# Two heads' attention scores on the two row halves of the matrix array, in a two-layer float32 trunk

## The chip, the core and the metric

One core of a Trainium2 chip runs the whole program. The metric is the device time of one execution in microseconds (us). The engines are PE (matrix products; its weight loads are listed as PEld), DVE and ACT (elementwise work; both read PE's accumulator banks), POOL (small elementwise work here) and SP, which issues the transfers. Every engine takes its instructions in the order in which the program lists them. Products land in accumulator banks, of which the kernel keeps eight of 128 x 512 float32.

## The reference

A trunk of two layers over 256 tokens of width 1024, all in float32. Layer 0 mixes tokens with eight stick-breaking heads and four differential heads (two softmax maps each), layer 1 with sixteen heads whose block choice, at 256 tokens, leaves plain causal softmax. All heads have 64 features, so a "pair" below is two heads (or the two maps of a differential head). Behind each mixer stand a squared-ReLU MLP and a gated embedding.

```python
z = jnp.einsum('bhqd,bhkd->bhqk', qi, k) * scale          # stick-breaking scores
s = jnp.einsum('bhqd,bhkd->bhqk', qi, ki) * scale         # each map of a differential head
s_own = jnp.einsum('bhqd,bhkd->bhqk', qi, k_own) * scale  # layer 1
...
h = h + squared_relu_mlp(rms_norm(h, mlp_norm[i]), w_ff1[i], w_ff2[i])
gate = jax.nn.sigmoid(rms_norm(h, ple_norm[i]) @ ple_gate[i])
h = h + gate * (p[i].astype(h.dtype) @ ple_proj[i])
```

There are 16 pairs: four stick-breaking, four differential, eight in layer 1.

## The kernel before

**Products.** A float32 product is made of three products in the format fp32r: each operand is split exactly into a high and a low part, and `mm3` issues high x high, high x low and low x high into one bank. Weights stream from memory in units of half a megabyte (`raw`), ACT writes their high part (`whi`), DVE the low part (`wlo`). The tokens stand as transposed activations `T0h`, `T0l`, `T1h`, `T1l`. Almost all of PE's work is this stream; attention is set between its products.

**Order.** Nothing is scheduled by the chip: a planner (`Order`) runs the tasks as generators, keeps a clock for each engine from cost formulas, and issues next the task of the highest rank whose wait is over by those clocks. So a changed cost or a changed wait in one task moves instructions of others too. Banks are taken from a pool of eight; side work such as attention holds at most five of them in layer 0 (`banks.room`).

**Scores.** Queries and keys of a pair lie on 128 partitions, head 0 on partitions 0 to 63 and head 1 on 64 to 127. A product over 128 partitions would add the two heads up. So one operand is kept zero-padded: the tiles `z` (high) and `zl` (low) are [128, pair, head, 256 tokens], and head 0's copy is zero on partitions 64 to 127, head 1's on 0 to 63. POOL writes the zeros (`z_tile`, lines 1184 and 1185), and the sinks `qk_sink` and `T_sink` write the two halves in two instructions of 64 partitions on ACT and again on DVE. A single product then gives both heads side by side in one bank.

- `soft` (a query tile t of 128 rows): t = 0 gives 2 x 128 columns, t = 1 gives 2 x 256, three products each. `diff_head` and `moba_pair` call it for t = 0 and t = 1 in turn; each call takes a bank, and DVE reads it (line 781) before the bank is given back.
- `stick_pair` (rows are keys): three products of 512 columns, a mask product in bfloat16 (256 columns), three of 256, another mask. Later it adds running sums of the softplus terms `sph`, `spl` by six products with the constant `negr`: two of 512 columns and four of 256.
- `average` (line 165) multiplies weights by values for two heads on the two column halves of the array: the tile is 128 rows by 64 columns, the two heads' products stand in turn in PE's list. It is plain float32, and each product appears as two records in the trace.

**The start.** POOL's list begins with the identity, then the zeros of layer 0, then the rotary tables from the token positions (`table_task`, tile `posi`), the norms (`rs_a`), the mask constants and the rotations of the first queries and keys (`rp`, `tok`).

Of the kernel before, what the change touches and what calls it, by code (L numbers as in the profile page):

```python
# [17 lines left out]
P = 128  # L18
# [29 lines left out]
# ---- order of issue: tasks are generators that yield what they wait for; the one of the  # L48
# highest rank whose wait is over by the clocks of the engines issues next ----
# [5 lines left out]
class Buffers:  # L55
    """Buffers that tasks take and give back."""
# [26 lines left out]
class Order:  # L83
# [66 lines left out]
    # -- instructions, each returning when its result can be read --  # L150
# [62 lines left out]
    def copy(self, out, in_, ps=False, scale=None, dep=0.0):  # L213
        """On the engine that is through with it first."""
# [13 lines left out]
def kernel(  # L228
# [65 lines left out]
    def constants_task():  # L294
# [5 lines left out]
        # rows are queries, columns keys: a key after its query is out  # L300
# [169 lines left out]
    class Norm:  # L470
        """rs = 1/rms, rs8 = rs/8, rs2 = 1/rms^2 of each token tile"""
# [10 lines left out]
    def transposes(nm, t, c, dep, calm=False):  # L482
        """h[t][:, c] -> acts"""
# [28 lines left out]
    def statistics(nm, t, pieces, need):  # L512
        """pieces of the row: (first column, columns, event)"""
# [29 lines left out]
    def chunk(acts, sink, tmajor=False):  # L543
        """512 output features, token-major; sink(t, bank) is a task"""
# [29 lines left out]
    def chunk_T(acts, sink):  # L574
        """512 output features on partitions, 128 at a time; sink(f2, bank) is a task for two such blocks"""
# [22 lines left out]
    def qk_sink(nm, dst, ev, eighth, padded):  # L598
        def sink(t, bk, dep):
# [22 lines left out]
            ts_ = slice(t * P, (t + 1) * P)  # L622
# [16 lines left out]
    def rows_task(nm):  # L639
        """1/rms of each token along the columns, on every partition"""  # L640
# [9 lines left out]
    def T_sink(dst, evs_, eighth, padded):  # L650
        def sink(f2, bk, dep):
# [7 lines left out]
            js = slice(2 * f2, 2 * f2 + 2)  # L659
            if padded:  # L660
                parts = [(v[64 * g:64 * g + 64], [d[64 * g:64 * g + 64, js, g, :] for d in dst]) for g in range(2)]
            else:
                parts = [(v, [d[:, js, :] for d in dst])]
            for v_, (hi, lo) in parts:
                e = o.act(hi, v_, AF.Copy)
            yield e
            for v_, (hi, lo) in parts:
                e = o.tt(lo, v_, hi.bitcast(F32), ALU.subtract)
# [28 lines left out]
    def put_T(oo, dep, acts, j):  # L697
        """token-major oo [128, 2 x 128] -> 128 features of acts"""
# [14 lines left out]
    scores = [0, None]  # L713

    def scored():
        """a pair's scores are out"""
# [4 lines left out]
    def stick_pair(j, kT, qz, q_ev, k_ev, v, v_ev, acts):  # L721
        yield (q_ev[j // 2], k_ev[j // 2], mask_ev, big.wake)
        b1 = big.take()
        e = b1[1]
        yield lambda: banks.wake(2, side=True)
        ba, bb = banks.take(side=True), banks.take(side=True)
        pa, pb = ba[1], bb[1][:, :256]
        a3 = pa.rearrange("q (g n) -> q g n", g=2)
        b3 = pb.rearrange("q (g n) -> q g n", g=2)
# [5 lines left out]
        yield ea  # L735
        o.act(e[:, :512], pa, AF.Abs, ps=True)
        o.act(e[:, 512:], pb, AF.Abs, ps=True, dep=eb)
        o.act(e, e, AF.Exp, scale=-1.0)
        t = o.act(e, e, AF.Ln, bias=one)
        yield t  # L740
        o.stt(e[:, 512:], pb, 0.0, e[:, 512:], ALU.max, ALU.add)
        t = o.stt(e[:, :512], pa, 0.0, e[:, :512], ALU.max, ALU.add)
# [3 lines left out]
        t = o.act(sph, e, AF.Copy)  # L746
        yield t
        t = o.tt(spl, e, sph.bitcast(F32), ALU.subtract)
# [6 lines left out]
        sps.give(*b2, t2)  # L755
        yield t1
        t1 = o.act(e[:, :512], pa, AF.Exp, ps=True)
        t2 = o.act(e[:, 512:], pb, AF.Exp, ps=True)
        banks.give(*ba, t1, side=True)
        banks.give(*bb, t2, side=True)  # L760
        yield (t2, *v_ev)
        wa = e[:, :512].rearrange("q (g n) -> q g n", g=2)
        wb = e[:, 512:].rearrange("q (g n) -> q g n", g=2)
        yield from average(lambda g: wa[:, g, :], lambda g: wb[:, g, :], v, j * P, acts, j, b1)

# [1 line left out]
    def soft(j, t, qT, kz, q_ev, k_ev, e, st):  # L767
# [8 lines left out]
        if t == 1:  # L776
            scored()
# [509 lines left out]
```

## Time and profile before

| | |
|---|---|
| time, median of 3 runs (lowest to highest) | 676.93 us (676.45 to 677.07) |
| span of the profiled execution | 674.7 us |
| PE busy, share of the span | 656.8 us, 97% |
| PE weight loads | 569.6 us, 84% |
| DVE busy | 451.6 us, 67% |
| ACT busy | 417.1 us, 62% |
| POOL busy | 61.9 us, 9% |
| granted clock of PE, mean | 0.998 of full speed |

The span runs from the first to the last recorded instruction; no own time of the profiled execution stands beside it, and the median of the timed runs is 2.2 us longer than the span. A matmul record lasts longer than the step to the next one, since products are pipelined: what a product costs PE is read from the distance between the starts of records that follow each other, not from their durations.

### The profile page before, as it was taken

The page shows a single profiled execution, that of the slowest core. Times are in us where ns is not written, and L with a number is a line of the kernel's source. Part 1 is how long each engine was busy: PE and PEld are TensorE (multiplying, and loading weights), DVE is VectorE, ACT ScalarE, POOL GpSimd, SP SyncE. Part 2 cuts the span into 40 slices and gives each one's busy share as a digit, 9 for nine tenths or more (in the row PEclk, how much of TensorE's full clock was granted, in tenths as well). Part 3 has the DMA queues.
Part 4 walks back from the last instruction along what each step waited for, and adds up shares of the span by engine and source line. Part 5 has one row for each costly group of instructions (what it writes and reads, how often), then busy time and mean ns, then how long its engine had stood idle before and what let it go on. Part 6 is the DMA issues. An engine that isn't in the chain of part 4 may idle for free.

```text
span 674.7 us, 10997 instructions
## 1 busy us (share of the span) xinstructions
PE 656.8 (97%) x3906; PEld 569.6 (84%) x3906; DVE 451.6 (67%) x936; ACT 417.1 (62%) x886; POOL 61.9 (9%) x129
## 2 busy tenths in 40 slices
PE   6799999999999999999999999999999999999995
PEld 4589878899998999898887777778998999899885
DVE  6789767777456554666895776758657545655584
ACT  7667887675446553655796776758646544655482
POOL 8820001000000000000043022000000000000010
PEclk9999999999999999999999999999999999999999
DMA  7753643456466546754656434435476546654621
GB/s 256 219 202 93 199 130 114 133 170 227 150 223 218 169 153 210 229 173 140 198 184 197 139 113 145 156 94 176 146 242 207 167 149 226 219 169 150 211 95 62
DMA packets 50054, 115.61 MB, mean 171 GB/s; under 512 B 4000, under 2 KB 5456, under 8 KB 50000
## 3 DMA queue, kind: packets, MB, share of 16 engines
q1 hardware_dynamic: 49824, 114.39, 52.0%
q8 instruction: 30, 0.49, 0.3%
q0 software_dynamic: 176, 0.53, 0.3%
q14 instruction: 24, 0.20, 0.1%
HBM read 113.86 MB, written 1.05 MB: 170 GB/s over the span
## 4 chain that ended last, share of the span: by engine, by line
PE 83%; issue 8%; POOL 7%; ACT 0%; DVE 0%; POOLq 0%; DVEq 0%; ACTq 0%
PE bank L159 80%; POOL rp L196 3%; PE bank L170 2%; PE bank L165 1%; POOL tok L196 1%; POOL prod L1102 1%; POOL rem L1103 1%; ACT tok L178 0%; POOL zl L1184 0%; POOL z L1185 0%; POOL z L1184 0%; POOL zl L1185 0%; POOL ang L1092 0%; POOL rs_a L527 0%; POOL rs_f L527 0%
## 5 line engine op out<-in xcount | busy, mean ns | idle before, releaser
L192 DVE TENSOR_TENSOR wlo<-raw,whi 128x512 fp32r<-128x512 f32 x424 | 276.9, 696 | 89.1 <-ACT whi L178 63.5
L178 ACT ACTIVATE whi<-raw 128x512 fp32r<-128x512 f32 x424 | 243.7, 628 | 97.9 <-PE bank L159 71.9
L159 PE MATMUL bank<-T0h,whi 128*128 128x256 f32 x576 | 161.7, 281 | 0.0
L159 PE MATMUL bank<-whi,hid 128*128 128x512 f32 x512 | 161.4, 391 | 0.0
L159 PE MATMUL bank<-T0l,whi 128*128 128x256 f32 x576 | 160.8, 279 | 0.0
L159 PE MATMUL bank<-T0h,wlo 128*128 128x256 f32 x576 | 160.7, 279 | 0.0
L159 PEld LDWEIGHTS bank<-whi,hid 128*128 128x128 f32 x512 | 96.1, 188 | 19.7
L159 PEld LDWEIGHTS bank<-T0h,whi 128*128 128x128 f32 x576 | 108.2, 188 | 0.7
L159 PEld LDWEIGHTS bank<-T0l,whi 128*128 128x128 f32 x576 | 107.8, 187 | 0.7
L159 PEld LDWEIGHTS bank<-T0h,wlo 128*128 128x128 f32 x576 | 108.2, 188 | 0.0
L159 PE MATMUL bank<-wlo,hid 128*128 128x512 f32 x256 | 99.6, 389 | 0.0
L192 DVE TENSOR_TENSOR tok<-tok 128x512 f32<-128x512 f32 x32 | 22.1, 690 | 67.1 <-ACT tok L178 67.1
L159 PE MATMUL bank<-whi,T0h 128*128 128x512 f32 x160 | 66.1, 413 | 0.2
L159 PE MATMUL bank<-wlo,T0h 128*128 128x512 f32 x160 | 63.7, 398 | 0.5 <-DVE wlo L192 0.4
L159 PE MATMUL bank<-whi,T0l 128*128 128x512 f32 x160 | 63.4, 396 | 0.0
L178 ACT ACTIVATE tok<-bank 128x512 f32<-128x512 f32 x32 | 18.8, 589 | 71.9 <-PE bank L159 71.9
L159 PEld LDWEIGHTS bank<-wlo,hid 128*128 128x128 f32 x256 | 48.1, 188 | 9.4
L159 PE MATMUL bank<-whi,T1h 128*128 128x512 f32 (+1 forms) x136 | 53.8, 396 | 0.0
L159 PE MATMUL bank<-whi,T1l 128*128 128x512 f32 (+1 forms) x136 | 51.8, 381 | 0.0
L159 PE MATMUL bank<-wlo,T1h 128*128 128x512 f32 (+1 forms) x136 | 51.8, 381 | 0.0
L527 POOL TENSOR_TENSOR rs_p<-ms_p,pexp 128x1 f32<-128x1 f32 x4 | 2.2, 552 | 436.0 <-DVE ms_p L209 436.0
L159 PEld LDWEIGHTS bank<-wlo,T0h 128*128 128x128 f32 x160 | 30.2, 189 | 7.7 <-DVE wlo L192 1.8
(161 smaller groups left out, 737.3 us busy)
## 6 DMA issues: line engine op xcount, KB each, us to landing
raw<-in_w_ff_dram SPq DMA_DIRECT2D x128, 512.0 KB, 4.4
raw<-in_moba_w_in_dram SPq DMA_DIRECT2D x24, 512.0 KB, 4.4
raw<-in_ab_w_in_dram SPq DMA_DIRECT2D x23, 512.0 KB, 4.7
raw<-in_ple_gate_dram SPq DMA_DIRECT2D x16, 512.0 KB, 4.7
raw<-in_ab_w_out_dram SPq DMA_DIRECT2D x8, 512.0 KB, 4.5
raw<-in_moba_w_out_dram SPq DMA_DIRECT2D x8, 512.0 KB, 3.3
raw<-in_ple_proj_dram SPq DMA_DIRECT2D x4, 512.0 KB, 3.3
h<-in_x_dram SPq DMA_DIRECT2D x4, 256.0 KB, 5.6
```

The costliest lines, as they stand in the source:

```text
L159: self.nc.tensor.matmul(out, lhsT, rhs, start=start, stop=stop, **kw)
L165: self.nc.tensor.matmul(out, lhsT, rhs, start=start, stop=stop)
L170: self.nc.tensor.transpose(out, in_, ident)
L178: self.nc.scalar.activation(out, in_, func, **kw)
L192: self.nc.vector.tensor_tensor(out, a, b, op=op)
L196: self.nc.gpsimd.tensor_tensor(out, a, b, op=op)
L527: nc.gpsimd.tensor_tensor(nm.rs[:, t:t + 1], b, pexp[:, 0:1], op=ALU.pow)
L1102: nc.gpsimd.tensor_scalar(prod, k, -c, None, op0=ALU.mult)
L1103: nc.gpsimd.tensor_tensor(dst, prod, src, op=ALU.add)
```

## The change

The padded tiles go. `z` becomes [128, high/low, pair, 256 tokens] and `zl` is dropped; no zeros are written, and each sink writes its result in one ACT and one DVE instruction. A new `mm3_heads` issues the three products head by head in turn, each over 64 partitions (`head_rows`): head 0 uses rows 0 to 63 of the array and writes one bank, head 1 rows 64 to 127 and another bank. `scores_of` takes two banks and issues both query tiles at once; `soft` then reads them. In `stick_pair` each head has its own bank of 384 columns, so masks and running sums come a head at a time: four masks of 128 columns, and eight products with `negr`, four of 384 and four of 128 columns.

```diff
+    def mm3_heads(self, steps, first=True):
+
+        for a, b, start, stop in ((0, 0, first, False), (0, 1, False, False), (1, 0, False, True)):
+            for out, l_, r_ in steps:
+                self.nc.tensor.matmul(out, l_[a], r_[b], start=start, stop=stop, skip_group_check=not first)
+                e = self.spend("pe", max(0.5 * width(r_[b]) / 2.4, 55.0) + 6)
+        return e
...
-            if padded:
-                parts = [(v[64 * g:64 * g + 64], [d[64 * g:64 * g + 64, :, g, ts_] for d in dst]) for g in range(2)]
-            else:
-                parts = [(v, [d[:, :, ts_] for d in dst])]
-            for v, (hi, lo) in parts:
-                e = o.act(hi, v, AF.Copy, ps=True)
+            hi, lo = [d[:, :, t * P:(t + 1) * P] for d in dst]
+            e = o.act(hi, v, AF.Copy, ps=True)
             yield e
-            for v, (hi, lo) in parts:
-                e = o.tt(lo, v, hi.bitcast(F32), ALU.subtract)
+            e = o.tt(lo, v, hi.bitcast(F32), ALU.subtract)
...
+    def head_rows(x, j, g, c0, c1):
+
+        return [d[64 * g:64 * g + 64, j, c0:c1] for d in x]
...
-        mm3(a3, kT[0][:, j, 0:P], kT[1][:, j, 0:P], qz[0][:, j, :, :], qz[1][:, j, :, :], True, False)
-        ea = o.mm(a3[:, :, 0:P], identb, smask, False, True)
-        mm3(b3, kT[0][:, j, P:256], kT[1][:, j, P:256], qz[0][:, j, :, P:256], qz[1][:, j, :, P:256], True, False)
-        eb = o.mm(b3, identb, smask, False, True)
+        bs = [banks.take(side=True) for _ in range(2)]
+        ps = [b[1] for b in bs]
+        o.mm3_heads([(ps[g][:, :256], head_rows(kT, j, g, 0, P), head_rows(q, j, g, 0, 256)) for g in range(2)])
+        o.mm3_heads([(ps[g][:, 256:384], head_rows(kT, j, g, P, 256), head_rows(q, j, g, P, 256)) for g in range(2)],
+                    first=False)
+        ws = []
+        for g in range(2):
+            for c in (0, 256):
+                w = o.mm(ps[g][:, c:c + P], identb, smask[:, 0], False, True, skip_group_check=True)
+            ws.append(w)
...
-        for s_ in (sph, spl):
-            o.mm(pa, negl, s_[:, :512], False, False, skip_group_check=True)
-            t1 = o.mm(a3[:, :, P:256], negone, s_[:, 512:].rearrange("q (g n) -> q g n", g=2), False, s_ is spl,
-                      skip_group_check=True)
-            t2 = o.mm(pb, negl, s_[:, 512:], False, s_ is spl, skip_group_check=True)
...
+        for g in range(2):
+            for s_ in (sph, spl):
+                sg = s_.rearrange("q (g n) -> q g n", g=2)[:, g]
+                o.mm(ps[g][:, :384], negl, sg, False, False, skip_group_check=True)
+                w = o.mm(ps[g][:, P:256], negone, sg[:, 256:384], False, s_ is spl, skip_group_check=True)
+            ws.append(w)
...
+    def scores_of(j, q, k, q_ev, k_ev):
+
+        yield (*q_ev, *k_ev, mask_ev)
+        yield lambda: banks.wake(2, side=True)
+        bs = [banks.take(side=True) for _ in range(2)]
+        ws = [o.mm3_heads([(bs[g][1][:, P * t:P * t + P * (t + 1)], head_rows(q, j, g, P * t, P * (t + 1)),
+                            head_rows(k, j, g, 0, P * (t + 1))) for g in range(2)]) for t in range(2)]
...
-        w = mm3(s3, qT[0][:, j, ts_], qT[1][:, j, ts_], kz[0][:, j, :, 0:n], kz[1][:, j, :, 0:n], True, True)
...
-    def z_tile(name, layer, j):
...
-            for y in (z, zl[j]) if layer == 0 else (z,):
-                nc.gpsimd.memset(y[64:128, :, 0, :].bitcast(F32), 0.0)
-                nc.gpsimd.memset(y[0:64, :, 1, :].bitcast(F32), 0.0)
-                o.spend("pool", 1800)
...
+    def z_tile(name):
+
+        z = zpool.tile([P, 2, 4, 256], F32R, tag="z", name=name)
+        return z[:, 0], z[:, 1]
```

How PE's list changes shows best in layer 1 around two pairs of averages and scores. In these rows `big` and `v` are weights and values of an average (64 output partitions: a column half), `z`, `zl`, `sT` and `sl` keys and queries, `whi` and `T0h` the weight stream. Before:

```order
L165 MATMUL bank_72<-big_95,v_3257 64x256 x2
L165 MATMUL bank_72<-big_95,v_3257 64x128 x2
L159 MATMUL bank_74<-z_3255,sT_3258 128x256
L159 MATMUL bank_74<-zl_152,sT_3258 128x256
L159 MATMUL bank_74<-z_3255,sl_150 128x256
L165 MATMUL bank_75<-big_97,v_3257 64x256 x2
L165 MATMUL bank_75<-big_97,v_3257 64x128 x2
L159 MATMUL bank_69<-z_3255,sT_3258 128x256
L159 MATMUL bank_69<-zl_152,sT_3258 128x256
L159 MATMUL bank_69<-z_3255,sl_150 128x256
L159 MATMUL bank_76<-whi_83,T0h 128x512
```

The same place in the changed kernel, with the products of line 173 on row halves:

```order
L165 MATMUL bank_69<-big_93,v_3303 64x256 x2
L165 MATMUL bank_69<-big_93,v_3303 64x128 x2
L173 MATMUL bank_74<-z_3301,sT_3304 128x128
L173 MATMUL bank_76<-z_3301,sT_3304 128x128
...
L173 MATMUL bank_74<-z_3301,sl_150 128x256
L173 MATMUL bank_76<-z_3301,sl_150 128x256
L165 MATMUL bank_73<-big_96,v_3303 64x256 x2
L165 MATMUL bank_73<-big_96,v_3303 64x128 x2
L173 MATMUL bank_75<-z_3301,sT_3304 128x128
L173 MATMUL bank_72<-z_3301,sT_3304 128x128
```

A pair's scores now stand in one piece of twelve products on two banks, where three products of one query tile stood, and the array's halves are taken by columns and by rows in turn.

POOL's list at the start, before (`z` and `zl` are the padded tiles, `posi` the positions):

```order
L1185 MEMSET z_169 64x4x256
L1184 MEMSET zl_153 64x4x256
L1185 MEMSET zl_153 64x4x256
L1089 MEMSET invf 128x1 x8
L1090 CAST posf<-posi 128x2
```

And now:

```order
masks.py:197 MEMSET ident 128x128
masks.py:199 ISA
masks.py:199 AFFINE_SELECT ident<-ident 128x128
L1096 MEMSET invf 128x1 x8
L1097 CAST posf<-posi 128x2
```

The cast of the positions, which eight memsets stood ahead of, now follows the identity; the rest of POOL's list up to the first rotation is as it was.

## Rows read from the trace of the kernel before

**Rows 1.** The page: busy engines, PE's granted clock by slices, the chain.

```profile
PE 656.8 (97%) x3906; PEld 569.6 (84%) x3906; DVE 451.6 (67%) x936; ACT 417.1 (62%) x886; POOL 61.9 (9%) x129
...
PEclk9999999999999999999999999999999999999999
...
PE 83%; issue 8%; POOL 7%; ACT 0%; DVE 0%; POOLq 0%; DVEq 0%; ACTq 0%
```

**Rows 2.** Waits of PE: us in total, times, longest.

```profile
PE bank L170 <- POOL tok L196: 3.0, 5, 1.3
PE bank L159 <- POOL rs_a L527: 1.6, 1, 1.6
PE bank L159 <- DVE wlo L192: 0.4, 2, 0.2
```

**Rows 3.** PE's timeline: start us, us, line, operation, out<-in, count; a score block.

```profile
50.08 0.28 PE L159 MATMUL bank<-T0h,whi 128*128 128x256 f32 x1
...
50.43 0.39 PE L159 MATMUL bank<-z,sT 128*128 128x512 f32 x1
...
51.13 0.28 PE L159 MATMUL bank<-T0h,whi 128*128 128x256 f32 x1
```

**Rows 4.** PE's groups by form: count, busy us and mean ns of one.

```profile
L159 PE MATMUL bank<-z,sT 128*128 128x512 f32 x16 | 6.6, 414 | 0.0
...
L159 PE MATMUL bank<-z,sT 128*128 128x256 f32 x16 | 5.3, 334 | 0.0
...
L159 PE MATMUL bank<-v,big 128*128 128x128 f32 x24 | 3.0, 275 | 0.0
```

**Rows 5.** PE's timeline around the two column halves of an average.

```profile
100.02 0.40 PE L159 MATMUL bank<-whi,T0l 128*128 128x512 f32 x1
100.35 0.87 PE L165 MATMUL bank<-big,v 128*64 128x256 f32 x8
101.15 0.50 PE L159 MATMUL bank<-whi,T0h 128*128 128x512 f32 x1
101.49 0.40 PE L159 MATMUL bank<-wlo,T0h 128*128 128x512 f32 x1
```

**Rows 6.** The same average's first records: products begun by 100.36, loads begun by 100.5.

```profile
100.35 0.44 PE L165 MATMUL bank<-big,v 128*64 128x256 f32 x2
...
100.34 0.20 PEld L165 LDWEIGHTS bank<-big,v 128*64 128x64 f32 x4 [0.36 <-issue]
```

**Rows 7.** Weight loads by form: count, busy us and mean ns of one.

```profile
L159 PEld LDWEIGHTS bank<-z,sT 128*128 128x128 f32 x32 | 6.1, 190 | 1.2 <-issue 0.7
...
L165 PEld LDWEIGHTS bank<-big,v 128*64 128x64 f32 x96 | 5.8, 136 | 4.0 <-issue 1.2 <-ACT whi L178 0.4
```

**Rows 8.** The chain in order of time: a run of transposes, 128 columns each.

```profile
351.52 0.87 PE bank L170 x8
```

**Rows 9.** PE's timeline: running sums of one stick-breaking pair, between weight products.

```profile
97.23 0.62 PE L159 MATMUL bank<-sph,negr 128*128 128x512 f32 x3
97.69 0.63 PE L159 MATMUL bank<-spl,negr 128*128 128x512 f32 x3
98.16 0.39 PE L159 MATMUL bank<-whi,T0h 128*128 128x512 f32 x1
```

**Rows 10.** POOL's timeline at the start; the positions' transfer (issue, then us to landing).

```profile
9.62 0.95 POOL L1185 MEMSET zl<- 64x1024 f32 x1
...
10.80 0.43 POOL L1090 CAST posf<-posi 128x2 f32<-128x2 int32 x1
...
L394 SPq DMA_DIRECT2D posi<-in_positions_dram x1: 612/612/612, 4.2 to 4.2; - x1
...
DMA to landing us min/median/max: 6.2/6.2/6.2
```

**Rows 11.** DVE's halves of the padded tile (min/median/max ns); the fullest stretch of DVE.

```profile
L192 DVE TENSOR_TENSOR zl<-bank,z x12: 681/688/695, 43.4 to 419.3; 64x512 fp32r<-64x512 f32 x12
...
51.00:68.00 17.00, 17.00 (x143) 16.47 (x142) 16.36 (x45) 12.11 (x32) 0.00 (x0) 1.00 0.31 93
```

More of the change, by code (lines that the diff above doesn't have):

```diff
@@ L596, with qk_sink @@
     rope_ev = Event()
-    def qk_sink(nm, dst, ev, eighth, padded):
+    def qk_sink(nm, dst, ev, eighth):
         def sink(t, bk, dep):
@@ L658, in sink @@
             yield e
[L659 to L665, printed above, removed]
+            hi, lo = [d[:, 2 * f2:2 * f2 + 2, :] for d in dst]
+            e = o.act(hi, v, AF.Copy)
             yield e
-            for v_, (hi, lo) in parts:
-                e = o.tt(lo, v_, hi.bitcast(F32), ALU.subtract)
+            e = o.tt(lo, v, hi.bitcast(F32), ALU.subtract)
             toks.give(ti, tok, e)
@@ L719, in scored, with stick_pair @@
             scores[1].t = o.now
-    def stick_pair(j, kT, qz, q_ev, k_ev, v, v_ev, acts):
+    def head_rows(x, j, g, c0, c1):
+        return [d[64 * g:64 * g + 64, j, c0:c1] for d in x]
+    def stick_pair(j, kT, q, q_ev, k_ev, v, v_ev, acts):
         yield (q_ev[j // 2], k_ev[j // 2], mask_ev, big.wake)
         b1 = big.take()
-        e = b1[1]
+        e = b1[1].rearrange("q (g n) -> q g n", g=2)
         yield lambda: banks.wake(2, side=True)
[L726 to L729, printed above, removed]
-        mm3(a3, kT[0][:, j, 0:P], kT[1][:, j, 0:P], qz[0][:, j, :, :], qz[1][:, j, :, :], True, False)
-        ea = o.mm(a3[:, :, 0:P], identb, smask, False, True)
-        mm3(b3, kT[0][:, j, P:256], kT[1][:, j, P:256], qz[0][:, j, :, P:256], qz[1][:, j, :, P:256], True, False)
-        eb = o.mm(b3, identb, smask, False, True)
-        scored()
[L735 to L739, printed above, removed]
+        bs = [banks.take(side=True) for _ in range(2)]
[8 more added lines that the diff above has]
+            ws.append(w)
+        scored()
+        yield ws[0]
+        for g in range(2):
+            o.act(e[:, g], ps[g][:, :384], AF.Abs, ps=True, dep=ws[g])
+        o.act(b1[1], b1[1], AF.Exp, scale=-1.0)
+        t = o.act(b1[1], b1[1], AF.Ln, bias=one)
         yield t
-        o.stt(e[:, 512:], pb, 0.0, e[:, 512:], ALU.max, ALU.add)
-        t = o.stt(e[:, :512], pa, 0.0, e[:, :512], ALU.max, ALU.add)
+        for g in range(2):
+            t = o.stt(e[:, g], ps[g][:, :384], 0.0, e[:, g], ALU.max, ALU.add)
         yield (t, sps.wake)
@@ L755, in stick_pair @@
[L755 to L767, printed above, removed]
-        n = (t + 1) * P
-        yield (q_ev[t], *k_ev[:t + 1], mask_ev)
-        yield lambda: banks.wake(side=True)
-        bs = banks.take(side=True)
-        s3 = bs[1][:, :2 * n].rearrange("q (g k) -> q g k", g=2)
-        ts_ = slice(t * P, (t + 1) * P)
-        w = mm3(s3, qT[0][:, j, ts_], qT[1][:, j, ts_], kz[0][:, j, :, 0:n], kz[1][:, j, :, 0:n], True, True)
-        if t == 1:
-            scored()
-        yield w
-        for g in range(2):
-            nc.vector.tensor_tensor_reduce(e[:, g, :], s3[:, g, :], cmask[:, P * (1 - t):], -1.0, 3.0e38, ALU.add, ALU.min,
-                                           accum_out=st[:, g:g + 1])
-            w = o.spend("dve", 130 + 1.04 * n)
-        banks.give(*bs, w, side=True)
@@ new lines, in stick_pair @@
+        ws = []
+        for g in range(2):
+            for s_ in (sph, spl):
[3 more added lines that the diff above has]
+            ws.append(w)
+        sps.give(*b2, w)
+        yield ws[0]
+        for g in range(2):
+            t = o.act(e[:, g], ps[g][:, :384], AF.Exp, ps=True, dep=ws[g])
+            banks.give(*bs[g], t, side=True)
@@ new lines, in stick_pair @@
+        yield (t, *v_ev)
+        yield from average(lambda g: e[:, g, :256], lambda g: e[:, g, 256:], v, j * P, acts, j, b1)
+    def scores_of(j, q, k, q_ev, k_ev):
[4 more added lines that the diff above has]
+                            head_rows(k, j, g, 0, P * (t + 1))) for g in range(2)]) for t in range(2)]
+        scored()
+        return bs, ws
@@ L785, in soft @@
+    def soft(t, bs, ws, e, st):
+        n = (t + 1) * P
+        yield ws[t]
+        for g in range(2):
+            nc.vector.tensor_tensor_reduce(e[:, g, :], bs[g][1][:, P * t:P * t + n], cmask[:, P * (1 - t):], -1.0, 3.0e38,
+                                           ALU.add, ALU.min, accum_out=st[:, g:g + 1])
+            w = o.spend("dve", 130 + 1.04 * n)
+        if t == 1:
+            for b in bs:
+                banks.give(*b, w, side=True)
         yield w
@@ L798, in diff_head @@
         sts = [tinies.take(), tinies.take()]
-        w = 0.0
         es = []
+        bs, ws = yield from scores_of(j, qT, kz, q_ev, k_ev)
         for t in range(2):
@@ L803, in diff_head @@
             st = sts[t][1]
-            w = yield from soft(j, t, qT, kz, q_ev, k_ev, e, st)
+            w = yield from soft(t, bs, ws, e, st)
             yield lam_ev
@@ L852, in moba_pair @@
         aT = ba[1].rearrange("q (g a n) -> q g a n", g=2, a=3)
+        bs, ws = yield from scores_of(j, qT, kz, q_ev, k_ev)
         for t in range(2):
@@ L856, in moba_pair @@
             e = be[1][:, 256 * t:256 * t + n].rearrange("q (g k) -> q g k", g=2)
-            yield from soft(j, t, qT, kz, q_ev, k_ev, e, st)
+            yield from soft(t, bs, ws, e, st)
             for g in range(2):
@@ L1176, in p_task @@
         pT_ev.t = e
-    def z_tile(name, layer, j):
-        z = zpool.tile([P, 4, 2, 256], F32R, tag="z", name=name)
-        def zeros():
-            yield o.now if layer else 1500.0
-            for y in (z, zl[j]) if layer == 0 else (z,):
-                nc.gpsimd.memset(y[64:128, :, 0, :].bitcast(F32), 0.0)
-                nc.gpsimd.memset(y[0:64, :, 1, :].bitcast(F32), 0.0)
-                o.spend("pool", 1800)
-        o.add(zeros(), 14)
-        return z, zl[j]
+    def z_tile(name):
+        z = zpool.tile([P, 2, 4, 256], F32R, tag="z", name=name)
+        return z[:, 0], z[:, 1]
     sl = [cst.tile([P, 4, 256], F32R, name=f"sl{j}") for j in range(2)]
-    zl = [cst.tile([P, 4, 2, 256], F32R, name=f"zl{j}") for j in range(2)]
     def trunk():
@@ L1202, in trunk @@
             banks.room[0] += 5 - banks.room[0] if i == 0 else 1
-            z = [z_tile(f"z{i}{j}", i, j) for j in range(2)]
+            z = [z_tile(f"z{i}{j}") for j in range(2)]
             v = vpool.tile([P, 2, D], F32, tag="v", name=f"v{i}")
```

19 lines of the change are left out of this document (9 added, 10 removed).

## The prediction

> **What bounds the kernel now.** First the page: PE is busy 97% of the span and the chain that ended last is PE for 83%, at a granted clock that never leaves its upper level of 2.4 GHz (the mean is 0.998) [rows 1]. Then PE's waits, to see whether it starves anywhere: the largest after the start are 3.0 us for rotated queries and keys and 1.6 us for `rs_a`, both POOL's, and 0.4 us for split weights [rows 2]. None is for a softmax result. So in the attention stretches PE is the limit, and what counts is how many microseconds of PE's own pitch the change adds or removes; ACT and DVE count only if PE begins to wait for them.
>
> The pitch comes from PE's timeline. In a score block, records of 256 columns follow at 0.117 us (50.08 to 50.43, three of them) and three of 512 take 0.70 us (50.43 to 51.13), so 0.233 each [rows 3]. The means of 414 and 334 ns [rows 4] are latencies of pipelined products and are not used.
>
> **What the zero-padding costs.** There are 16 rows each of the high-by-high products of 512 and of 256 columns [rows 4]; with the other two of each three that is 48 and 48. 48 x 0.233 + 48 x 0.117 = 16.8 us of PE. That is all that scores take now, 2.5% of the span, so the gain is bounded by half of it.
>
> **The new score products.** They are 192 half-array products, in 96 couples: 48 of 256 columns a head, 48 of 128. No row of before shows two row halves. The nearest is `average`, which uses two column halves: two products begin by 100.36 and end together 0.44 us after the first began, and four of their loads are over 0.20 us after the first began [rows 6]. The eight records take 0.80 us (100.35 to 101.15) [rows 5]; one after another, four at 2 x 0.109 and four at 0.109 (the pitch of 128-column float32 passes: eight transposes in 0.87 us [rows 8]) would take 1.31. So column halves do run side by side, and I take the same of row halves. What a couple then costs has a floor from weight loads: a load of 64 columns lasts 136 ns, one of 128 columns 190 [rows 7], so 64 more columns cost 54 ns and 128 columns stream in about 107 (an estimate from these two rows). Row halves load 128 columns each, column halves only 64. A wide couple, then, costs 0.12 us, the pitch of one 256-column product and a few ns for the second; a narrow one 0.11, the pitch of the transposes and about the load. 48 x 0.12 + 48 x 0.11 = 11.0 us. Gain: 16.8 - 11.0 = 5.8 us. From below, a narrow couple could go at 0.06 (half of 0.117, if loads of halves don't bind); from above, each product of a couple takes its own turn, 0.117 and 0.11, and the scores take 48 x (0.234 + 0.22) = 21.8 us.
>
> **The running sums.** Now 0.93 us a pair (97.23 to 98.16) [rows 9], 3.7 us for four. After: per pair four products of 384 columns, 0.175 each between the two pitches, and four of 128, which are fp32r and 128 columns wide and of which before has none; at 0.11 the pair takes 1.14, four take 4.6. Loss: 0.8 us. At 0.06 it is nothing; at 0.22 (below) it is 2.6. The mask products keep their columns (512 in bfloat16 a pair), so I cost them at nothing, and up to 0.8 us if each of the 16 is held to a load.
>
> **Changing between whole array and halves.** This is what the product count hides. The visit to the column halves at 100.35 begins 0.33 us after the last 512-column product instead of 0.233, its eight records take 0.80 instead of 0.65 (two couples of 0.218 and two of 0.109), and the first product behind it holds its follower off by 0.34 instead of 0.233 [rows 5]: 0.36 us for a visit, 0.18 for each of its two changes. In PE's list of before there are 11 visits (22 changes); in the list of after, counting every step between whole array, column halves and row halves, 45: 13 visits to row halves hold the 16 pairs (some hold two), and where an average stands between two of them the change is shared. 23 more changes x 0.18 = 4.1 us, and 13 entries wait for a load of 128 instead of 64 columns, 13 x 0.054 = 0.7. Loss: 4.8 us, the largest unknown: from nothing, if row halves need no change of that kind, to this.
>
> The Trainium skill's page "TensorEngine Tiling (Array Packing)", section "Key Properties", says that a change of tiling mode, other than a change of tile within a mode, drains the engine. It gives no figure; by it the row halves pay as the column halves do, which is the 4.8 us taken above, and without it the sum would end 4.8 us lower. The trace agrees for column halves with 0.36 us a visit; no row here shows it for row halves.
>
> **POOL's zeros at the start.** Eight memsets of some 0.95 us go, the last at 9.62 us, and the work behind them on POOL is what PE waits for, 1.6 + 3.0 us [rows 2, 10]. That looks like 8 x 0.95 = 7.6 us off POOL's start. It isn't: the next step needs the positions, whose transfer is issued at 4.2 and lands 6.2 us later, at 10.4; the cast began at 10.80 [rows 10]. The chain moves by 10.8 - 10.4, some 0.3 us with a semaphore's time. Gain 0.3 us, between 0 and 0.4. The four memsets of layer 1 keep nobody waiting and count nothing.
>
> **ACT and DVE.** Eight sinks lose one ACT and one DVE instruction each; a DVE one lasts 688 ns, and DVE is 96% busy from 51 to 68 us [rows 11]. PE does not wait there, so this is 0, and it is the cover for PE being faster. Banks: a pair now holds two from the first score to DVE's last reading, so a later pair's scores may stand later in the list. The planner charges nothing for changes, so PE will run behind its clocks rather than ahead, and results will be there when PE comes: 0, up to 1 us of new waits.
>
> **Sum.** 5.8 - 0.8 - 4.8 + 0.3 = 0.5 us gained. The profiled span of 674.7 becomes 674.2, and with the 2.2 us between span and median, kept as they are, the time is 676.4 us. A measurement of this kernel can tell about 0.2%, 1.35 us, from no change; this is no change. The likeliest case's own range is 674.5 to 678.5: couples some ns dearer or cheaper (96 x 0.01 = 1 us), masks 0.8, waits 1.
>
> **The rivals.**
>
> *Slower: the two heads don't go side by side.* Place: each of the 96 couples. If loads or streams of the two row halves take turns, a couple costs 0.214 (two loads) to 0.234, and instead of a gain of 5.8 the scores lose 3.7 to 5.0; with sums, changes and POOL that is 9 to 10 us more, about 686 us. It decides early: the change is a loss as soon as a couple averages over (16.8 - 0.8 - 4.8 + 0.3)/96 = 0.120 us, and one that can be measured over 0.134. For it: no row shows two row halves, and their loads are twice as long as those that rows 6 show together. Against it: rows 5 and 6. Chance 18%.
>
> The page "TensorE: Matmul & The Clock Gate", section "The mechanism", says that a load overlaps products in flight only where the row group differs. By that, each half's load would stand between its own products, and a wide couple would cost 0.107 + 0.117, so it is this rival. The trace differs for column halves: four loads are over while the first two products still run [rows 6].
>
> *Slower: narrow fp32r products run at the rate of plain float32.* A plain float32 product of 128 columns appears as two passes (24 records for 12 products [rows 4]) of 0.11 us. At 0.22 the 48 narrow couples and 16 narrow sums cost 64 x 0.11 = 7 us more: 683.5 us. For it: the kernel before keeps every fp32r product at 256 columns or more, so the trace can't exclude it. Chance 12%.
>
> *Faster: row halves change for nothing.* The 4.8 us stay out: 671.6 us. For it: row halves write all 128 columns, and nothing shows that the wait at 100.35 is the array's layout and not the column halves alone. Chance 14%.
>
> *Faster: narrow products at 0.06.* 64 x 0.05 = 3.2 us: 673.2 us. Against it: the load estimate of 107 ns. Chance 6%.
>
> **How the numbers follow.** The forecast has 50%; by its spread about a fifth of that lies below 675.6 and a twentieth above 678.3. Faster by over 0.2%: 0.10 + 0.14 + 0.06 = 0.30. Slower by over 0.2%: 0.02 + 0.18 + 0.12 = 0.32. Within: 0.38. The range leaves out the 18% of heads in turn and takes in the rest: 671.5 to 684.
>
> **What would show it.** The start of two half products of a couple within some ns and the next couple 0.11 to 0.12 us later shows the side-by-side step; starts 0.11 apart show the slower rival. The distance from the last weight product to the first half product, and from the last half product to the weight product's follower, gives the price of a change: 0.33 and 0.34 after 512-column products if I am right. The `negr` products of 128 columns show the narrow rate by themselves, on the whole array. The cast of the positions should start at about 10.5 us. I am wrong if couples are below 0.10 or above 0.13, if the 13 visits cost under 0.15 us each, or if PE shows new waits for ACT or DVE in the attention stretches.

## The result and the profile after

The changed kernel takes **686.72 us** (median of 4 runs, 684.96 to 688.20) against 676.71 us (676.45 to 677.07) for the kernel before beside it: ratio 1.0145, 95% interval 1.0129 to 1.0162. It is slower, where no change was forecast, and outside the range. The profiled execution of after is the slowest of its four (688.2 us, span 686.3): its mean granted clock is 0.990, that of the others 0.992 to 0.993. So the 11 to 12 us found in its trace below are more than the 10.0 us between the medians.

The page of after: engines busy, TensorE's granted clock by slices. The rows of before are [rows 1].

```profile
PE 662.0 (96%) x4018; PEld 572.7 (83%) x4018; DVE 443.2 (65%) x929; ACT 411.9 (60%) x877; POOL 49.6 (7%) x117
...
PEclk9999999989999999999999999999999999999998
```

DVE, ACT and POOL do less, as intended. PE has more busy time, and one slice of its clock is no longer full. PE's waits in after (us in total, times, longest), the answer to [rows 2]:

```profile
PE bank L159 <- DVE T0h L511: 3.2, 2, 2.6
PE bank L178 <- POOL tok L204: 3.0, 5, 1.3
PE bank L178 <- DVE T1l L200: 2.0, 1, 2.0
PE bank L159 <- POOL rs_a L535: 1.0, 1, 1.0
PE bank L159 <- ACT whi L186: 0.9, 1, 0.9
PE bank L159 <- ACT pp L186: 0.9, 1, 0.9
```

Four of these groups are new, on DVE and ACT. The wait for `whi` lies in the start, at 12.7 us, and the shorter of the two for `T0h` (0.6 us) in layer 1. The other three, 2.6, 2.0 and 0.9 us, lie between 105 and 147 us: 5.5 us of new waits in layer 0, ahead of its MLP. To find where the time went, take a landmark that both kernels have: PE's first and last product with `hid`, the MLP's hidden features (the two times before the semicolon). Before, then after:

```profile
L159 PE MATMUL bank<-whi,hid x512: 388/389/477, 161.2 to 643.8; 128*128 128x512 f32 x171
```

```profile
L159 PE MATMUL bank<-whi,hid x512: 388/389/477, 172.6 to 655.4; 128*128 128x512 f32 x171
```

The first such product comes 11.4 us later and the last 11.6 us later. So all of the loss lies in layer 0 ahead of its MLP; layer 1, with half of all score pairs, costs what it cost to 0.2 us. Two stretches there, windows of before and then of after (length, busy time and count of PE, PEld, DVE, ACT, POOL, PE's granted clock, DMA share, GB/s):

```profile
102.00:119.00 17.00, 17.00 (x99) 14.20 (x98) 13.26 (x44) 12.38 (x40) 2.12 (x3) 1.00 0.34 114
140.00:160.00 20.00, 20.00 (x173) 20.00 (x172) 12.38 (x23) 10.45 (x21) 0.00 (x0) 1.00 0.54 185
```

```profile
102.00:119.00 17.00, 14.09 (x91) 10.73 (x90) 9.74 (x27) 12.76 (x31) 1.49 (x3) 0.90 0.14 46
140.00:160.00 20.00, 17.02 (x105) 15.60 (x104) 13.67 (x31) 12.06 (x31) 0.00 (x0) 0.83 0.48 159
```

Idle time is 17.00 - 14.09 + 20.00 - 17.02 = 5.9 us. The clock takes 17 x 0.10 + 20 x 0.17 = 5.1 us more, of which 0.2 fall at the end of the second idle and are counted there: 4.9. Together 10.8 of the 11.4. Narrower windows of after show where the clock fell to its lower level of 1.2 GHz (0.50):

```profile
108.00:110.00 2.00, 2.00 (x9) 1.55 (x8) 1.97 (x4) 1.16 (x3) 0.00 (x0) 0.73 0.00 0
110.00:112.00 2.00, 2.00 (x7) 1.68 (x6) 0.75 (x2) 0.00 (x0) 0.00 (x0) 0.50 0.11 17
112.00:114.00 2.00, 2.00 (x20) 1.79 (x19) 0.13 (x1) 1.26 (x3) 0.00 (x0) 0.92 0.72 243
...
147.00:150.00 3.00, 3.00 (x13) 2.83 (x14) 2.83 (x11) 2.80 (x6) 0.00 (x0) 0.50 0.86 298
150.00:153.00 3.00, 3.00 (x16) 3.00 (x16) 2.17 (x4) 0.00 (x0) 0.00 (x0) 0.50 0.39 134
```

Each time PE had stood idle shortly before, for 2.0 and 2.6 us. PE's timeline of after at the second idle:

```profile
142.28 0.40 PE L159 MATMUL bank<-whi,pT 128*128 128x512 f32 x1
143.05 1.25 PE L178 MATMUL bank<-ident,h 128*128 128x128 f32 x8 [0.37 <-DVE h L200]
146.91 0.58 PE L159 MATMUL bank<-T0h,whi 128*128 128x256 f32 x1 [2.61 <-DVE T0h L511]
```

Eight transposes of the residual `h` stand in a row, and nothing is left for PE while ACT and DVE turn them into `T0h`. On DVE four low parts of weights stand ahead of the `T0h` that PE waits for, and the chain that ended last runs through them. DVE's timeline of after:

```profile
144.16 2.49 DVE L200 TENSOR_TENSOR wlo<-raw,whi 128x512 fp32r<-128x512 f32 x4
146.57 0.29 DVE L511 CAST T0h<-tok 128x256 fp32r<-128x256 f32 x1
```

In the kernel before, PE's timeline at the same step reads:

```profile
134.17 0.60 PE L170 MATMUL bank<-ident,h 128*128 128x128 f32 x4
134.52 0.48 PE L159 MATMUL bank<-whi,pT 128*128 128x512 f32 x1
...
135.31 0.60 PE L170 MATMUL bank<-ident,h 128*128 128x128 f32 x4
```

There the products with `pT` (the embedding, needed much later) stand around the transposes and go on to 138.55, a cover of 3 us. In after the planner has spent most of them from 116 us on. The reason stands earlier still. In a row-half block, one that begins with 128 columns is a softmax pair, one that begins with 256 a stick-breaking pair. PE's timeline of after:

```profile
65.37 0.44 PE L173 MATMUL bank<-z,sT 64*128 64x128 f32 x4
...
77.31 0.51 PE L173 MATMUL bank<-z,sT 64*128 64x256 f32 x4
```

At 65.4 us comes the fourth differential pair (I call the four D0 to D3), which in the kernel before came last, at 105.5. The sticks' scores are dated by their mask products. Before, then after:

```profile
L159 PE MATMUL bank<-smask,identb x8: 282/283/283, 67.5 to 91.5; 128*128 128x256 bf16 x8
```

```profile
L159 PE MATMUL bank<-smask,identb x16: 219/219/230, 78.2 to 114.2; 128*128 128x128 bf16 x16
```

Before, the sticks ran two at a time from 67 to 92 us; after, one at a time from 77 to 114. My theory: **D3 got in ahead of the sticks, took two of the five working tiles `big`, and left room for one stick at a time**. Long chains on ACT and DVE then stood alone, PE ran dry, and the idle brought the clock down. What let D3 in was the sinks: with one ACT and one DVE instruction each by the planner's clocks, D2's softmax is through, and its tile free, before the last stick's keys are out. (That the sinks tip the order is tested below; the way there, by the planner's clocks, is my reading of the code and not shown.) The rival: the row halves themselves, or the changes between whole array and halves, cost it.

### The profile page after: what moved, and what is told of

Same layout as the page of the kernel before. It is cut to its first block, busy times and chain, and to the rows that moved or that the text cites. A ratio compares the mean times of both kernels' runs of the same rounds, so it can differ in the third digit from the quotient of the medians.

```text
span 686.3 us, 11190 instructions
## 1 busy us (share of the span) xinstructions
PE 662.0 (96%) x4018; PEld 572.7 (83%) x4018; DVE 443.2 (65%) x929; ACT 411.9 (60%) x877; POOL 49.6 (7%) x117
## 4 chain that ended last, share of the span: by engine, by line
PE 83%; POOL 5%; issue 4%; DVE 3%; ACT 2%; DMA 1%; SPq 0%; POOLq 0%; DVEq 0%; ACTq 0%
PE bank L159 78%; PE bank L178 3%; POOL rp L204 2%; PE bank L173 2%; DVE wlo L200 1%; PE bank L165 1%; DMA posi<-in_positions_dram 1%; POOL tok L204 1%; POOL prod L1109 1%; ACT big L186 1%; DVE h L200 1%; POOL rem L1110 1%; ACT junk L186 0%; ACT tok L186 0%; DVE T0l L200 0%
## 5 line engine op out<-in xcount | busy, mean ns | idle before, releaser
L200 DVE TENSOR_TENSOR wlo<-raw,whi 128x512 fp32r<-128x512 f32 x424 | 277.4, 693 | 98.2 <-ACT whi L186 77.3
L159 PE MATMUL bank<-T0h,whi 128*128 128x256 f32 x576 | 163.5, 284 | 3.2 <-DVE T0h L511 3.2
L159 PEld LDWEIGHTS bank<-whi,T0h 128*128 128x128 f32 x160 | 30.3, 189 | 8.3 <-ACT whi L186 1.4
L159 PEld LDWEIGHTS bank<-whi,T0l 128*128 128x128 f32 x160 | 30.3, 189 | 7.2
```

What stands on the lines that cost most here:

```text
L200: self.nc.vector.tensor_tensor(out, a, b, op=op)
```

## The experiments

**The order alone (e1).** D3 is held until a stick pair's scores are out; all else is as changed.

```diff
+    late = Event()
+
     def scored():
 
         scores[0] -= 1
+        if scores[0] == 1 and late.t is None:
+            late.t = o.now
...
-    def diff_head(j, qT, kz, q_ev, k_ev, v, v_ev, acts):
+    def diff_head(j, qT, kz, q_ev, k_ev, v, v_ev, acts, after=0.0):
+        yield (after, q_ev[0], k_ev[0])
...
-                    o.add(diff_head(j, sT[1], z[1], evs["bq"], evs["bk"], v, evs["bv"], oacts), 22)
+                    o.add(diff_head(j, sT[1], z[1], evs["bq"], evs["bk"], v, evs["bv"], oacts, late if j == 3 else 0.0), 22)
```

> The changed kernel with one thing more: the fourth softmax pair of the first group (D3) may not ask for its score banks before a stick pair's scores are out, which puts TensorE's order in layer 0 back to nearly that of the kernel before (D3 last, sticks two at a time), while row halves, banks and sinks stay as changed. Theory order (the 10 us come from D3 getting in ahead of the stick pairs, which then run one at a time and leave TensorE idle at 105 and 144 us): 675 to 678 us, the first product of the MLP of layer 0 at 161 to 162.5 us of the span instead of 172.64, idle gaps of TensorE near the 8.2 us of before, clock 1.00 throughout. Rival row halves (their products, or the changes between whole and half array, cost it): stays at 685 to 688.

Measured: 675.94 us, ratio 0.9988 (0.9978 to 0.9997), span 674.1. The sticks and PE's two stretches in its trace:

```profile
L159 PE MATMUL bank<-smask,identb x16: 218/220/231, 66.7 to 89.8; 128*128 128x128 bf16 x16
```

```profile
102.00:119.00 17.00, 17.00 (x107) 14.26 (x106) 13.54 (x44) 12.62 (x41) 2.34 (x4) 1.00 0.40 126
140.00:160.00 20.00, 20.00 (x173) 20.00 (x172) 12.38 (x24) 10.43 (x21) 0.00 (x0) 1.00 0.56 185
```

The whole loss of 10.8 us is gone with every row-half product in place. The rival falls.

**The same order on the padded kernel (e2).** The stick pairs wait for D3's first scores; the products are those of before.

```diff
     def stick_pair(j, kT, qz, q_ev, k_ev, v, v_ev, acts):
+        yield early
...
+            if j == 3 and t == 0:
+                early.t = o.now
```

> The kernel before, zero-padded tiles and all, with one thing more: the stick pairs wait until the first query tile's scores of D3 are out, so that D3 runs ahead of them as in the changed kernel. Theory order: slower than before by most of the 10 us, 683 to 688 us, with idle of TensorE of 2 us or more in front of products between 100 and 147 us and a granted clock of 0.5 behind one or both of them. Rival row halves: 676 to 678, since every product is that of before.

Measured: 685.65 us, 1.0130 (1.0115 to 1.0146). Its sticks run one at a time too (masks from 79.8 to 113.3 us). Without one row half, the order costs 9.1 us, where the change cost 10.0. One part was missed: the idle comes in shorter pieces, and in this profile the clock stays up behind them. That holds for the profiled execution alone, the shortest of the four (684.05 us, mean clock 0.994): the other three are 1.6 to 2.6 us longer, with mean clocks of 0.990 to 0.992, and no trace shows where theirs fell. PE's timeline of this run:

```profile
141.75 1.25 PE L170 MATMUL bank<-ident,h 128*128 128x128 f32 x8 [1.06 <-DVE h L192]
143.81 0.39 PE L159 MATMUL bank<-T0h,whi 128*128 128x256 f32 x1 [0.81 <-DVE T0h L503]
...
146.17 0.38 PE L159 MATMUL bank<-T0h,whi 128*128 128x256 f32 x1 [1.05 <-DVE T0h L503]
```

**What tipped the order (e3).** The sinks write their halves in two instructions again.

```diff
-            hi, lo = [d[:, :, t * P:(t + 1) * P] for d in dst]
-            e = o.act(hi, v, AF.Copy, ps=True)
+            ts_ = slice(t * P, (t + 1) * P)
+            if not eighth:
+                parts = [(v[64 * g:64 * g + 64], [d[64 * g:64 * g + 64, :, ts_] for d in dst]) for g in range(2)]
...
+            for v, (hi, lo) in parts:
+                e = o.act(hi, v, AF.Copy, ps=True)
```

> The changed kernel, but the sinks of the keys and queries that were padded write their two halves with two ACT and two DVE instructions again, as before (same bytes, 16 more instructions in all of a layer). Theory order: these instructions are what held D3 back, so D3 is last again and it gets 675 to 679 us, though ACT and DVE do more work. Rival row halves: 686 to 689, as the changed kernel or worse by the added work.

Measured: 681.20 us, 1.0068 (1.0053 to 1.0084), between the two expectations. In layer 0 the theory holds: the order is back, and the first `hid` product is at 160.7. More work on ACT and DVE made this layer 12 us shorter. The miss is layer 1, where the same edit moved tasks too; PE's timeline there:

```profile
463.63 1.26 PE L178 MATMUL bank<-ident,h 128*128 128x128 f32 x8 [0.47 <-DVE h L200]
467.50 0.38 PE L159 MATMUL bank<-T0h,whi 128*128 128x256 f32 x1 [2.61 <-DVE T0h L511]
```

It is the same picture, eight transposes without cover, 2.6 us of idle, and behind it a clock of 0.56 for 2.5 us and 0.80 for 3 us: 2.6 + 1.1 + 0.6 = 4.3 us.

**The clock (e4).** Idle PE is filled with products that add zeros or are overwritten; the numbers count PE's products.

```diff
+        if self.pe == 752:
+            self.fill(out, 21, True)
         self.nc.tensor.matmul(out, lhsT, rhs, start=start, stop=stop, **kw)
+        if self.pe == 581:
+            self.fill(out, 16, False)
```

> The changed kernel with 37 products more that add zeros or are overwritten: 16 behind the product after which TensorE idles from 105.2 us, 21 in front of the one before which it idles from 144.0 us (1.9 and 2.5 us of work by 0.118 each). Order, waits and row halves stay. Theory clock by idle: about 5 us of the loss is the 1.2 GHz level behind the two idles, so with the idle filled the clock stays 1.00 and the time falls to 680 to 683. Rival clock by other means (the half-array products or transposes themselves pull it down): clock 0.5 stays, 686 to 688.

Measured: 683.93 us, 1.0109 (1.0094 to 1.0124); the windows of this run:

```profile
102.00:119.00 17.00, 16.00 (x109) 12.73 (x108) 10.90 (x26) 12.97 (x29) 1.34 (x2) 1.00 0.15 40
140.00:160.00 20.00, 19.38 (x152) 17.92 (x151) 15.76 (x34) 14.07 (x33) 0.00 (x0) 1.00 0.60 190
```

The clock stays up with every row-half product and transpose in place, so in after it was the idle that brought it down. The first `hid` product comes at 168.6 instead of 172.6, 4.0 us of the 4.9. The median gains 2.8 us and is 0.9 above the expectation; the two profiled executions, the slowest of after and the fastest of this kernel, lie 4.8 apart.

**Room instead of order (e6).** Seven tiles `big` (`N_BIG = 7` for 5), and nothing holds D3 back.

> The changed kernel with seven working tiles named big instead of five and nothing held back: D3 still runs ahead of three of the stick pairs, but these find two tiles and run two at a time. Theory order, in the form that the shortage of working tiles behind D3 is what spreads the sticks out: 675 to 679 us, no idle of 2 us at 105 or 144 us. Rival D3 ahead is bad by itself: 683 to 687.

Measured: 676.67 us, 1.0000 (0.9991 to 1.0009); masks from 68.4 to 91.7 us. D3's scores now stand at 55.9 us, ahead of all four sticks, and the first two sticks follow at 67.6 and 68.8, where after has its first at 77.3. So D3 ahead does no harm when two sticks still fit; with the two more tiles D3 itself came earlier, and this run does not part the two.

**Do the halves run side by side? (e5, e9)** Two runs on the kernel with D3 held. The first writes the products head by head:

```diff
-        for a, b, start, stop in ((0, 0, first, False), (0, 1, False, False), (1, 0, False, True)):
-            for out, l_, r_ in steps:
+        for out, l_, r_ in steps:
+            for a, b, start, stop in ((0, 0, first, False), (0, 1, False, False), (1, 0, False, True)):
```

> The kernel of e1_d3_late, with the products of a pair's scores written head by head (three of head 0, then three of head 1) and not in couples; same 192 products, same order of all else on every engine. If couples run side by side, as their starts 3 to 4 ns apart say, the 96 couples of 0.109 to 0.12 us become 192 products of 0.107 to 0.12 us one behind the other: 10 to 11 us longer than e1, 686 to 687 us. If the start times in the records mislead and a couple takes its time for another reason, within 1 us of e1, 675 to 677.

Measured: 675.88 us, 0.9988 (0.9979 to 0.9997): no difference to the couples, against my theory as I had put it. Either the couples did nothing, or the order in the list does not matter. The second run tells them apart:

```diff
-        return [d[64 * g:64 * g + 64, j, c0:c1] for d in x]
+        return [d[0:64, j, c0:c1] for d in x]
```

> The kernel of e1_d3_late with head 1's scores left out: both products of a couple use head 0's 64 rows, each into its own bank; order and instructions as e1. If e5 was as fast as e1 because each half of the array works through its own products by itself, then 192 products on one half have to stand one behind the other: 96 x 0.11 to 0.118 us more, 686 to 687 us. If a product of 64 rows simply takes half the time of one of 128, whichever half it uses, it stays at 675.5 to 676.5.

Measured: 687.40 us, 1.0157 (1.0139 to 1.0175), 11.5 us above the kernel with D3 held. Some of that is clock: the two executions with the highest mean clock (0.996 and 0.997) are 10.5 and 10.8 us above it, the other two (0.994), one of them profiled, 12.1 and 12.6. PE's timeline of the first block of 24, with both heads on the same rows:

```profile
45.95 0.66 PE L173 MATMUL bank<-z,sT 64*128 64x128 f32 x4
46.45 0.38 PE L173 MATMUL bank<-z,sl 64*128 64x128 f32 x2
46.67 0.69 PE L173 MATMUL bank<-z,sT 64*128 64x256 f32 x4
...
48.91 0.38 PE L159 MATMUL bank<-T0h,whi 128*128 128x256 f32 x1
```

With the heads in turn, each on its own half:

```profile
45.85 0.44 PE L173 MATMUL bank<-z,sT 64*128 64x128 f32 x4
46.13 0.29 PE L173 MATMUL bank<-z,sl 64*128 64x128 f32 x2
46.24 0.46 PE L173 MATMUL bank<-z,sT 64*128 64x256 f32 x4
...
47.44 0.38 PE L159 MATMUL bank<-T0h,whi 128*128 128x256 f32 x1
```

2.96 us on one half, 1.59 on two. So halves do run side by side. The clock of the profiled execution fell behind the third such block on one half, which took from 425.92 to 428.87 us; no idle over 0.3 us stands near it, and behind the first two blocks (at 45.95 and 377.39) the clock stayed up. Windows there:

```profile
428.00:430.00 2.00, 2.00 (x11) 1.67 (x11) 1.73 (x7) 1.50 (x8) 0.00 (x0) 0.75 0.01 2
430.00:432.00 2.00, 2.00 (x7) 1.51 (x6) 1.09 (x6) 0.07 (x1) 0.00 (x0) 0.50 0.50 147
```

And in e5 the starts leave the order of the list: in PE's list the third product is head 0's `z,sl`, but the trace has four `z,sT` first, two of each head, and then both `z,sl`. Each half takes up its own products, although three of the other half's stand ahead of them; in the unrounded records the starts come in pairs 10 ns apart, which I read as head 0 and head 1, instead of 3 in couples. So for the two halves the opening section's sentence that every engine takes its instructions in the order of the list does not hold.

**The price of a change (e10, e11).** A whole-array product of 128 columns that adds zeros, 16 times: inside a pair's scores, or behind them.

```diff
+            if whole == b and a == 0:
+                self.nc.tensor.matmul(steps[0][0][:, :P], self.zeros, self.zeros, start=False, stop=False, skip_group_check=True)
```

> The kernel of e1_d3_late with one product more in each of the 16 pairs, over the whole array and 128 columns, that adds zeros, behind the second couple of a pair's scores: two changes between row halves and whole array more in each pair. If a visit costs 0.385 us, as the records around the visits of e1 say, this adds 16 x 0.385 = 6.2 us and 16 products of about 0.11, 1.8 us: 683 to 685 us. If changes are free, 677 to 678.

> The control for e10_break_visits: the same 16 products, each behind the last couple of its pair, where the array changes to whole anyway in 13 of 16 places. 1.8 us for the products and 3 x 0.385 us for the three places inside a visit of two pairs: 677.5 to 679.5 us, some 5 us below e10. If changes are free, as e10.

Measured: 682.63 us (1.0088, 1.0072 to 1.0104) and 679.12 us (1.0037, 1.0023 to 1.0051), 6.7 and 3.2 above the kernel with D3 held. One pair, first with the product inside (`fill`), then without it (D3 held):

```profile
56.12 0.44 PE L173 MATMUL bank<-z,sT 64*128 64x128 f32 x4
56.49 0.33 PE L176 MATMUL bank<-fill 128*128 128x128 f32 x1
56.74 0.33 PE L173 MATMUL bank<-z,sl 64*128 64x128 f32 x2
...
57.41 0.55 PE L180 MATMUL bank<-ident,big 128*128 128x128 f32 x3
```

```profile
55.30 0.44 PE L173 MATMUL bank<-z,sT 64*128 64x128 f32 x4
55.58 0.28 PE L173 MATMUL bank<-z,sl 64*128 64x128 f32 x2
...
56.19 0.55 PE L178 MATMUL bank<-ident,big 128*128 128x128 f32 x3
```

1.29 against 0.89 us: 0.40 for the product and two changes, about 0.29 for the changes alone with 0.11 for the product; 16 x 0.40 = 6.4 of the 6.7 us. Changes are not free. The two runs lie 3.5 us apart, not 5: I had counted 13 places where the product behind meets a change anyway; in the trace there are 11 (two more stand ahead of an average), and 11 x 0.29 = 3.2.

**The zeros and the positions (e7, e8).** The positions' transfer is issued first, in the kernel with D3 held and, alone, in the kernel before.

```diff
+    posi = cst.tile([P, 2], I32, name="posi")
+    nc.sync.dma_start(posi, positions[0].rearrange("(t q) -> q t", q=P))
...
-                nc.sync.dma_start(posi, positions[0].rearrange("(t q) -> q t", q=P))
```

> The kernel of e1_d3_late with the transfer of the positions issued first on SP, not behind the first weights and inputs. If this transfer is what kept the zeros' removal from paying (POOL idle 7.2 us for it in e1), POOL's chain at the start moves forward by 1 to 2 us and so do TensorE's three waits for it (1.7, 1.5 and 0.6 us): 673 to 675 us. If not, 675.5 to 676.5 as e1.

> The kernel before with the positions' transfer issued first and nothing else. POOL is busy with the zeros until 10.5 us there, so an earlier landing can't be used: 676 to 677 us, no change. If the transfer alone were the limit, as much gained as e7 against e1, 1 to 3 us.

Measured: **673.46 us** (0.9952, 0.9935 to 0.9969), 2.5 below e1; and 677.01 us (1.0006, 0.9996 to 1.0015), no change. The cast of the positions on POOL, in the first of the two runs, then in the second:

```profile
L1102 POOL CAST posf<-posi x1: 187/187/187, 3.0 to 3.0; 128x2 f32<-128x2 int32 x1
```

```profile
10.81 0.43 POOL L1090 CAST posf<-posi 128x2 f32<-128x2 int32 x1
```

The zeros and the late transfer covered each other; only with both away does the start get shorter by more than the 0.7 us by which the cast moved in e1. PE's waits for POOL (`tok` and `rs_a`) fall from 4.6 us in e1 to 2.0, 2.6 less, for 2.5 gained. The kernel with both beats before and after: 0.5% faster than before.

## Why the prediction was wrong, step by step

- **Where PE is the limit.** Right for the kernel before, and taken over to the kernel after without support. PE waits 0.4 us in all for ACT or DVE [rows 2] while the order keeps cover beside such waits, as with the `pT` products above, and the order was about to change. One reading is off, and nothing hangs on it: the clock of before does leave its upper level, in the last 2.7 us of the span, which is the 0.002 that the mean lacks.
- **Score products.** Right. Couples follow at 0.11 and 0.12 us in the trace; the first of a wide row takes 0.16 to 0.17 and the first narrow one behind a wide row 0.06, so a block of 24 has 1.37 us in its 11 steps where 0.11 and 0.12 give 1.26. The floor from loads fits, too. The rival of heads in turn is refuted by e9, which shows its price (10.5 to 11.5 us); that it named 686 us, and 686.72 was measured, is chance. "Narrow at 0.06" falls with the couples. The Trainium skill's page "TensorEngine Tiling (Array Packing)", section "Key Properties", says that tiles work independently and that different tiles can load and multiply in parallel; e5 and e9 agree, with 1.59 us against 2.96.
- **Running sums.** 1.14 us a pair forecast; 1.10 where nothing disturbs (eight products from 79.30 to 80.40 us with D3 held), and the product behind them is held off by 0.05 more. In the unrounded records the next product starts 0.06 us after one of 128 columns, but that next one, of 384 columns, then takes 0.23 instead of 0.175, so 128 columns cost 0.11 as forecast. The rival of the plain float32 rate is refuted.
- **Changes.** 0.36 us a visit forecast, and 0.05 for the longer load. Around a visit that stands between whole-array products I read 0.385 with D3 held. Of that 0.11 are the slow first couples inside the block, above, which leaves 0.28 for the two changes; e10 says 0.29. The rival that they are free is refuted by e10 and e11.
- **POOL.** Right in kind: the transfer covers the zeros. The cast started at 10.86 in after and 10.08 with D3 held, since the landing varies (6.7 and 5.9 us after issue).
- **The sum.** 0.5 us of gain. With the order put back (e1), it is 0.7 us on the medians (675.94 against 676.60 beside it; by the interval, 0.2 to 1.5): the terms above held together. The 2.2 us between span and time set one execution's span beside another's time; in nearly every execution on record the two of one execution are 1.8 to 1.9 apart (688.2 and 686.3).
- **The step that failed** is "ACT and DVE": "PE does not wait there, so this is 0", and for new waits "0, up to 1 us". They were 5.5 us in layer 0 of after, with 4.9 us of slower clock behind the idle, for which the sum had no term at all. The reason given, that "results will be there when PE comes", took the order as fixed. I costed eight shorter sinks by what PE waits for, and not by what the planner does with results that are ready earlier: it gave D3 its tiles ahead of the sticks. I suspected the banks; e3 keeps the two banks a pair and still restores layer 0, so they were not what tipped it. The list of the changed kernel showed the new order before any run, but the two places that I drew from it were in layer 1 and at the start, where nothing went wrong.

I had named new waits for ACT or DVE in the attention stretches as the sign that I am wrong. That is what the profile shows at 105.6 us; the longest, at 144.3, stands just behind the attention.

What stays open: 0.6 of the 11.4 us in layer 0, and why filling the idle returns 4.0 of 4.9 us. Why the restored sinks cost 4.3 us in layer 1 (e3) is described above, not explained. Whether the planner could be given a rule that keeps the `pT` products as cover was not tried.

## What to carry to other kernels

Where a planner or a scheduler sets the order, a saving on an engine that nobody waits for is not worth nothing: it decides who gets the next buffer. Compare the whole sequence of tasks before and after, and look for tasks of one kind that ran in twos and now run one by one, and for a chain of other engines whose cover has been spent. Price idle of TensorE with the slower clock behind it, and after a slowdown change the order alone first.

## What the runs showed of the hardware

- Each half of the array's rows takes up its products by itself: with three products of the other half ahead in the list it starts 10 ns behind that half (e5, 675.88 against 675.94 us). The Trainium skill's page "TensorE: Matmul & The Clock Gate", section "The mechanism", says that products start and end strictly in the order of the program; the starts in e5 do not.
- Idle of 2.0 and 2.6 us in busy stretches was followed by the 1.2 GHz level, 4.9 us of loss behind 4.6 us of idle; filled with products that add zeros or are overwritten, the clock stayed at 1.00 (e4). Shorter idle went either way: pieces of 0.8 to 1.1 us left the clock at 1.00 in the profiled execution of e2, while 1.6 us near 23 us was followed by the lower level in the profiles of e2 and e8 and not in that of before.
- Idle is not the only way down: in e9 the clock was at 0.50 from 429.0 to 432.4 us behind 24 products on one half of the rows (2.95 us), with PE busy throughout. Two like blocks left it at 1.00.
- On one half, products of 128 columns follow at 0.12 us and of 256 at 0.13 (e9: 0.72 us for six, 0.77 for the next six), so a load does not stand between two products of the same rows. The same section of the Trainium skill says in its list that a load overlaps running products only where the row group differs, which would give over 0.2 for the wide ones (an estimate: 0.107 for the load, 0.118 for the columns); its text above the list also lets a load go ahead into a background weight buffer, and with that the 0.13 agrees. The measurement decides.
- The positions' transfer lands 2.1 us after its issue when issued first, at 0.8 us, and 5.9 to 6.7 us after it when issued at 4.1 to 4.2 us behind others (before, after and e1).
